# Dealing gathered row columns to the stretches of an expert mixer, and how far ahead they are fetched

## The chip, the cores and the metric

The kernel runs on one NeuronCore of one Trainium2 chip. The metric is the device time of one execution in microseconds; three runs of the kernel before are known. PE is TensorE, DVE VectorE, ACT ScalarE, POOL GpSimd, SP SyncE.

## The reference

One layer of a hybrid decoder for 336 tokens (256 prompt, 64 sample, 16 meta): a Conformer convolution branch and a Mamba-2 branch, joined and projected, and after them a PEER expert mixer. The change touches the mixer alone:

```python
def peer_block(xb, w_q, keys, U, V):
    q = (xb @ w_q).reshape(T, PEER_HEADS, 2, D_KEY // 2)
    s = jnp.einsum('thcd,hckd->thck', q, keys).astype(jnp.float32)
    s1, i1 = lax.top_k(s[:, :, 0], PEER_TOPK)
    s2, i2 = lax.top_k(s[:, :, 1], PEER_TOPK)
    ...
    sc, f = lax.top_k(cand, PEER_TOPK)
    ids = (jnp.take_along_axis(i1, f // PEER_TOPK, axis=-1) * N_KEYS
           + jnp.take_along_axis(i2, f % PEER_TOPK, axis=-1))
    g = jax.nn.softmax(sc, axis=-1)
    act = jax.nn.gelu(jnp.einsum('thkd,td->thk', U[ids], xb).astype(jnp.float32), approximate=False)
    w = (g * act).astype(xb.dtype)
    return jnp.einsum('thk,thkd->td', w, V[ids])
```

There are 8 heads with 16 experts each, so 128 experts a token out of 16384; U and V have 16384 rows of 1024.

## The kernel before, in words

The mixer treats its 320 tokens in two ways, side by side.

**Dense tokens.** 176 tokens go through all experts. The table U is read as 128 blocks of 128 experts (`u_block`, 512 KB each, tile `eraw`, fetched on SP's queue): PE multiplies a block with the tokens (L1272, tile `pj`), ACT applies gelu into S (L1274). Then V is read as 128 blocks (`v_block`), and PE adds S times a block into the accumulators `va` (L1366). Blocks are written here as U0 to U127 and V0 to V127. Between the two, S is weighted: `g_step` takes 8 tokens at a time, DVE builds one-hot tiles `oh` (L1293, L1294, L1296), PE multiplies them into `pg` (L1301), DVE multiplies `pg` into S (L1308). There are 22 such groups of 8 tokens for the first half of the experts (groups 0 to 21) and 22 for the second (22 to 43). Two `oh` buffers exist, so group n + 2 is built after group n is done.

**Gathered tokens.** 128 tokens (and 16 more, packed into 16 extra columns) fetch just the rows they need. A *column* is one expert for each of 128 partitions: `gather` has POOL issue an indirect DMA (L1083) of 128 rows of 8 KB, a U row and a V row side by side, into tile `wuv`. `pick_dot` has DVE take the dot product with the U half (L1195), ACT apply gelu and the gate (L1197, L1198, tile `scg`); `pick_sum` has DVE add the V half to `ygat` or `acce` (L1203). There are 144 columns and five `wuv` buffers (UV). `pick_row(n)` does the dot of column n and the sum of column n - 1; before the dot, `ahead(n)` issues the gathers that are wanted by then and not yet issued.

**What sets the order.** A `Feed` hands out such tasks between blocks: each block adds credit, and tasks are written into the program as the credit allows. There are four stretches: U0 to U87 beside the topk of the dense tokens (44 columns), U88 to U127 beside groups 0 to 21 (30), V0 to V63 beside groups 22 to 43 (42), and V64 to V126 beside nothing else (29 tasks: 28 columns and the last sum). A scheduler then settles each engine's row of instructions, so that a task need not stand where it was written. A gather issued at U88 or later also waits for a block's matmul:

```python
steps = ustep[SB:] + vstep
if len(steps) > LEAD:
    tc.add_manual_dep(i_.ins, steps[-1 - LEAD], ...)
```

that is, the block four before the one last written (LEAD is 4). SP fetches blocks into a ring of eight slots. Behind V126 `finish` normalizes and writes the gathered tokens, and `finish_dense` the others.

Of the kernel before, what the change touches and what calls it, by code (L numbers as in the profile page):

```python
# [42 lines left out]
NCOL = NPICK + (NPICK // XQ if NX else 0)  # L43
# [4 lines left out]
SB = 88  # L48
HB = 64
KTILES = ((0, NGAT), (128, 128), (256, 64))  # L50
NU = (44, 30, 42)
LM = (0.05, 0.05, 0.1, 0.5, 0.999)
LOW = 400
NW0 = 3
RB = 4
OH = 2
UV = 5
GLAG = 14
PLACE = (38, 50)
LASTP = 126  # L60
# [75 lines left out]
def body(tc, ia, oa, stop=None):  # L136
    nc = tc.nc
    with ExitStack() as top:
# [58 lines left out]
        def pj(name="pj"):  # L197
            return ps.tile([128, PJ], F32, name=name, tag="pj", bufs=3)[:, :T]
# [754 lines left out]
        def spread(row):  # L953
            u = gp.tile([128, 2 * D], F32, name="wuv", bufs=UV)[:, :D]
            nc.sync.dma_start(u, bass.AP(tensor=row.tensor, offset=row.offset, ap=[[0, 128], [1, D]]))
            return u
# [122 lines left out]
        ustep, vstep = [], []  # L1079

        def gather(c):
            u = gp.tile([128, 2 * D], F32, name="wuv", bufs=UV)
            i_ = nc.gpsimd.indirect_dma_start(out=u, out_offset=None, in_=ia["peer_uv"],  # L1083
                                              in_offset=bass.IndirectOffsetOnAxis(ap=gid[:, c:c + 1], axis=0))
            steps = ustep[SB:] + vstep
            if len(steps) > LEAD:
                tc.add_manual_dep(i_.ins, steps[-1 - LEAD], mybir.DependencyInfo(mybir.DependencyClass.Sync,
                                                                          mybir.DependencyReason.DATA),
                                  reason="rows after blocks")
            return u  # L1090

        def ahead(n):
            for i_ in range(n, min(n + UV - 1, NCOL)):
                if i_ not in pend:
                    pend[i_] = gather(COLS[i_])

        for j in range(16):
            w = weight(ia["w_q"], j)
            p = pj()
            proj(p[:, :T2], w, rows(ah[:, :, :T2], al[:, :, :T2]))  # L1100
            qT = qp.tile([128, T], F32, name="qT", bufs=3)
            nc.scalar.copy(qT[:, :T2], p[:, :T2])
            p = misc([128, 3, NK], "psc")
            for i, (t0, L) in enumerate(KTILES):
                nc.tensor.matmul(p[:L, i], qT[:, t0:t0 + L], keys[:, j, :], start=True, stop=True)  # L1105
                s_ = sall[:, i - 1, j] if i else kp.tile([128, NK], F32, name="sco", bufs=9)
                nc.scalar.copy(s_[:L], p[:L, i])
                if i == 0:
                    top16(sv[i], si[i], s_[:L], j)
            if j % (2 * HG) == 2 * HG - 1:  # L1110
                heads(j // 2 - HG + 1)
            if j == 2 * HG - 1:
                ahead(0)
# [77 lines left out]
        def pick_dot(n):  # L1191
            ahead(n)
            c, u = COLS[n], pend[n]
            w = scg[:, c:c + 1]
            nc.vector.scalar_tensor_tensor(u[:, :D], u[:, :D], 1.0, x2m if c < NPICK else x2e,  # L1195
                                           op0=OP.mult, op1=OP.mult, accum_out=w)
            nc.scalar.activation(w, w, AF.Gelu)  # L1197
            nc.scalar.activation(w, w, AF.Copy, scale=ggw[:, c:c + 1])  # L1198

        def pick_sum(n):  # L1200
            c, u = COLS[n], pend.pop(n)
            a_ = ygat if c < NPICK else acce
            nc.vector.scalar_tensor_tensor(a_, u[:, D:], scg[:, c:c + 1], a_, op0=OP.mult, op1=OP.add)  # L1203

        def group_sum():
            for c_ in range(2):
                p = misc([128, 512], "pgo")
                cs = slice(c_ * 512, c_ * 512 + 512)
                nc.tensor.matmul(p[:NX], C(f"sel{NX}"), acce[:, cs], start=True, stop=True)
                nc.scalar.copy(x2e[:NX, cs], p[:NX])  # L1210

        def pick_row(n):
# [4 lines left out]
            if n:  # L1217
                pick_sum(n - 1)
            if NX and n == XAT + NCOL - NPICK + GLAG:
                group_sum()  # L1220
# [3 lines left out]
        def take(n):  # L1224
            t = ops[:n]
            del ops[:n]
            return t

        def mixin(a_, b_):
            out, na, nb = [], len(a_), len(b_)  # L1230
            for q, t in enumerate(a_):
                out.append(t)
                out += b_[q * nb // na:(q + 1) * nb // na]
            return out

        t1, t2 = topk_tasks(1), topk_tasks(2)
        bg = mixin(t1[:-1] + t2[:-5] + t1[-1:] + t2[-5:-1], take(NU[0] - 4)) + take(4) + t2[-1:]

# [71 lines left out]
        def g_tasks(half):  # L1310
            return [(2.8, lambda t=t: g_step(half, t)) for t in range(0, ND, GT)]
# [8 lines left out]
        Sm.append(s1p.tile([128, 128 - SB, ND], F32, name="S1"))  # L1320
        feed = Feed(mixin(g_tasks(0), take(NU[1])), 128 - SB - 2)
        for b in range(SB, 128):
# [50 lines left out]
        def finish_dense():  # L1373
            yd = gp.tile([128, KD, ND], F32, name="nd")
            sqd = gp.tile([128, KD, ND], F32, name="sqd", tag="wuv", bufs=UV)
            pr = pj("prd")
# [11 lines left out]

        feed = Feed(mixin(g_tasks(1), take(NU[2])), HB - 2)
        for b in range(HB):  # L1390
# [109 lines left out]
```

## Time and profile before

| | |
|---|---|
| median of three runs | 1370.71 us (1370.0 to 1375.5) |
| the profiled execution | 1375.22 us, span 1373.5 |
| PE busy | 1319.4 us (96%), granted clock 0.983 |
| DVE, ACT, POOL busy | 1017.6, 526.4, 581.7 us |
| DMA | 382.05 MB, mean 278 GB/s; columns 151.00 MB on q0, blocks and the rest 227.46 MB on q1 |
| first U block, first V block, end of the last V block | 622.6, 996.3, about 1363 us into the span |

Busy times are sums over the whole span and say little about a stretch; the columns matter only from 622 us on, so the profile is read there, stretch by stretch. Matmuls of blocks are f32, and one of the program stands as two records in the profile: 16 records are one block. A wait is told as "engine, tile, line <- what ended it: us in total, times, longest".

### The profile page before, as it was taken

How to read it: one execution, taken by the hardware profiler on the slowest of the kernel's cores; microseconds unless marked ns; L12 is line 12 of the kernel's file. 1: busy time of each engine (PE TensorE's matmuls, PEld its weight loads, DVE VectorE, ACT ScalarE, POOL GpSimd, SP SyncE). 2: the span in 40 equal slices, each digit the busy share in tenths (PEclk: the TensorE clock that was granted, in tenths of full speed). 3: DMA queues.
4: the chain of work that ended last, by engine and by line, in shares of the span. 5: the costliest groups of instructions: out<-in, count | busy, mean ns of one | idle time of the engine just before them, and what ended most of it. 6: DMA issues, size and time to landing. Idle time of an engine off the chain costs nothing.

```text
span 1373.5 us, 24602 instructions
## 1 busy us (share of the span) xinstructions
PE 1319.4 (96%) x9324; PEld 1250.6 (91%) x9324; DVE 1017.6 (74%) x2340; ACT 526.4 (38%) x1393; POOL 581.7 (42%) x492
## 2 busy tenths in 40 slices
PE   9999999999999999998999988999999999987997
PEld 7888888888889999898998988999999999976897
DVE  7898777887866346799999885668787777766543
ACT  6777777777666434442222121111111111111101
POOL 2477776786746667542212331123222212344110
PEclk9999999999999999999999998999999999999999
DMA  6445545445344445439999999899999999999993
GB/s 237 160 127 171 166 160 162 142 149 187 108 142 127 150 154 165 148 114 380 398 413 393 409 416 362 288 416 363 372 416 415 380 377 390 395 417 416 414 412 113
DMA packets 87094, 382.05 MB, mean 278 GB/s; under 512 B 10144, under 2 KB 15648, under 8 KB 66368
## 3 DMA queue, kind: packets, MB, share of 16 engines
q1 hardware_dynamic: 65056, 227.46, 45.7%
q0 software_dynamic: 20736, 151.00, 27.3%
q10 hardware_dynamic: 1184, 2.02, 0.4%
q8 instruction: 73, 1.20, 0.3%
q14 instruction: 45, 0.37, 0.1%
HBM read 367.41 MB, written 13.03 MB: 277 GB/s over the span
## 4 chain that ended last, share of the span: by engine, by line
PE 77%; DVE 12%; DMA 8%; ACT 2%; issue 1%; POOL 0%; ACTq 0%; DVEq 0%
PE pj L150 30%; PE va L1366 19%; PE pj L1272 16%; DMA eraw<-in_vE_dram 5%; PE pg L1301 4%; PE pst L150 2%; DMA eraw<-in_uT_dram 2%; DVE wuv L1195 1%; DVE ygat L1203 1%; PE po L150 1%; PE py L150 1%; DVE pcv L473 1%; PE pdec L150 1%; PE ptr L155 1%; PE psc L1105 1%
## 5 line engine op out<-in xcount | busy, mean ns | idle before, releaser
L1083 POOL DMA_INDIRECT wuv<-in_peer_uv_dram,gid x144 | 183.0, 1271 | 523.4 <-DVE ygat L1203 159.7
L1272 PE MATMUL pj<-nd,eraw 128*128 128x176 f32 x2048 | 325.4, 320 | 11.5 <-DMA eraw<-in_uT_dram 7.6
L1366 PE MATMUL va<-S,eraw 128*128 128x176 f32 x2048 | 318.0, 315 | 18.9 <-DMA eraw<-in_vE_dram 18.9
L218 POOL TENSOR_TENSOR wl<-wraw,wh 128x1024 fp32r<-128x1024 f32 x111 | 267.2, 2408 | 149.7 <-ACT wh L217 78.0
L1366 PEld LDWEIGHTS va<-S,eraw 128*128 128x128 f32 x2048 | 307.6, 191 | 24.4 <-DMA eraw<-in_vE_dram 22.1
L1272 PEld LDWEIGHTS pj<-nd,eraw 128*128 128x128 f32 x2048 | 314.8, 195 | 13.5 <-ACT S L1274 8.8
L150 PE MATMUL pj<-ah,wh 128*128 128x336 f32 (+1 forms) x768 | 243.8, 329 | 0.7 <-ACT xnf L193 0.7
L150 PE MATMUL pj<-al,wh 128*128 128x336 f32 (+1 forms) x768 | 233.8, 318 | 0.0
L1203 DVE SCALAR_TENSOR_TENSOR ygat<-wuv,scg,ygat 128x1024 f32<-128x1024 f32 x128 | 163.9, 1280 | 57.8 <-ACT scg L1198 56.5
L1197 ACT ACTIVATE scg<-scg 128x1 f32<-128x1 f32 x144 | 29.0, 202 | 418.1 <-DVE wuv L1195 412.8
L1195 DVE SCALAR_TENSOR_TENSOR wuv<-wuv,x2m 128x1024 f32<-128x1024 f32 x128 | 156.0, 1218 | 42.6 <-DMA wuv<-in_peer_uv_dram,gid 42.6
L217 ACT CAST wh<-wraw 128x1024 fp32r<-128x1024 f32 x125 | 131.2, 1050 | 117.1 <-PE pj L150 79.9
L473 DVE SCALAR_TENSOR_TENSOR pcv<-ccat,vec,pcv 128x256 f32<-128x256 f32 x464 | 148.8, 379 | 17.1 <-ACT pcv L471 17.1
L150 PEld LDWEIGHTS pj<-ah,wh 128*128 128x128 f32 x768 | 147.1, 192 | 8.6 <-ACT xnf L193 2.7
L150 PEld LDWEIGHTS pj<-al,wh 128*128 128x128 f32 x768 | 146.5, 192 | 0.7
L150 PE MATMUL pj<-ah,wl 128*128 128x336 f32 (+1 forms) x768 | 137.0, 315 | 0.0
L150 PEld LDWEIGHTS pj<-ah,wl 128*128 128x128 f32 x768 | 120.5, 188 | 0.8 <-issue 0.7
L1274 ACT ACTIVATE S<-pj 128x176 f32<-128x176 f32 x128 | 37.6, 312 | 157.3 <-PE pj L1272 155.2
L1301 PE MATMUL pg<-oh 128*128 128x64 bf16 x1056 | 74.9, 242 | 0.0
L1308 DVE TENSOR_TENSOR S<-S,pg 128x192 f32<-128x192 f32 (+1 forms) x66 | 31.6, 506 | 56.9 <-PE pg L1301 56.9
L1301 PEld LDWEIGHTS <-oh 128*128 128x128 bf16 x1056 | 70.9, 117 | 2.2
L487 DVE SCALAR_TENSOR_TENSOR pj<-mcat,vec,pj 128x360 f32<-128x360 f32 x96 | 56.3, 588 | 3.6 <-ACT pj L485 3.6
(366 smaller groups left out, 1703.4 us busy)
## 6 DMA issues: line engine op xcount, KB each, us to landing
eraw<-in_uT_dram SPq DMA_DIRECT2D x128, 512.0 KB
eraw<-in_vE_dram SPq DMA_DIRECT2D x128, 512.0 KB
wraw<-in_w_in_dram SPq DMA_DIRECT2D x80, 512.0 KB
st<-in_state_dram SPq DMA_DIRECT2D x8, 1024.0 KB
out_ssm_s_dram<-st SPq DMA_DIRECT2D x8, 1024.0 KB
wraw<-in_w_mo_dram SPq DMA_DIRECT2D x16, 512.0 KB
wraw<-in_w_q_dram SPq DMA_DIRECT2D x16, 512.0 KB
wraw<-in_w_co_dram SPq DMA_DIRECT2D x8, 512.0 KB
```

The costliest lines, as they stand in the source:

```text
L150: i_ = nc.tensor.matmul(*a_, **kw)
L217: (nc.vector.tensor_copy if on_dve else nc.scalar.copy)(h, src)
L218: (nc.gpsimd if on_pool else nc.vector).tensor_tensor(l, src, h.bitcast(F32), op=OP.subtract)
L473: t = nc.vector.scalar_tensor_tensor(o, i_, wv, a_, op0=OP.mult, op1=OP.add)
L487: nc.vector.scalar_tensor_tensor(o, cat[:, w:w + n], wv, o, op0=OP.mult, op1=OP.add)
L1083: i_ = nc.gpsimd.indirect_dma_start(out=u, out_offset=None, in_=ia["peer_uv"], in_offset=bass.IndirectOffsetOnAxis(ap=gid[:, c:c + 1], axi ...
L1195: nc.vector.scalar_tensor_tensor(u[:, :D], u[:, :D], 1.0, x2m if c < NPICK else x2e, op0=OP.mult, op1=OP.mult, accum_out=w)
L1203: nc.vector.scalar_tensor_tensor(a_, u[:, D:], scg[:, c:c + 1], a_, op0=OP.mult, op1=OP.add)
L1272: i_ = nc.tensor.matmul(p[:, :ND], raw[:, k, :], nd[:, k, :], start=(k == 0), stop=(k == KD - 1))
L1274: nc.scalar.activation(Sv(b), p[:, :ND], AF.Gelu)
L1301: i_ = nc.tensor.matmul(pg[:, q, :], B[:, q // 4, :, q % 4], A[:, c_, q // 4, :, q % 4], start=(c_ == 0), stop=(c_ == 2))
L1366: i_ = nc.tensor.matmul(va[k // 2][:, k % 2], raw[:, k, :], Sv(b), start=False, stop=(b == 127), skip_group_check=True)
```

## The change

The columns are dealt 48, 30, 36 to the first three stretches, which leaves 31 tasks to the fourth. `ahead(n)` looked UV - 1 = 4 columns ahead (its own included) everywhere; now it does so while at most 64 V blocks are written (DEEP), and 2 from V64 on (NEAR): the dot of column n is written together with the gather of column n + 1.

```diff
-NU = (44, 30, 42)
+NU = (48, 30, 36)
 ...
 UV = 5
+DEEP = 4
+NEAR = 2
 ...
         def ahead(n):
-            for i_ in range(n, min(n + UV - 1, NCOL)):
+            for i_ in range(n, min(n + (DEEP if len(vstep) <= HB else NEAR), NCOL)):
                 if i_ not in pend:
                     pend[i_] = gather(COLS[i_])
```

Line numbers of the changed kernel are 2 higher in the mixer. POOL's row of instructions is unchanged; what its gathers wait for is not. Up to group 8 the rows of DVE, PE and ACT are unchanged too. The first place where they part is between groups 8 and 9. DVE's row there, before (a line with L1308 is a group's end, L1195 a column's dot, L1203 a sum):

```order
L1203 SCALAR_TENSOR_TENSOR ygat<-wuv,scg,ygat 128x1024
L1195 SCALAR_TENSOR_TENSOR wuv,scg<-wuv,x2m 128x1024
L1203 SCALAR_TENSOR_TENSOR ygat<-wuv,scg,ygat 128x1024
L1308 TENSOR_TENSOR S_7557<-S_7557,pg 128x64x8
L1293 TENSOR_TENSOR oh<-iorep,i2T 128x1024
L1294 TENSOR_TENSOR oh<-iorep,i1T 128x512
L1195 SCALAR_TENSOR_TENSOR wuv,scg<-wuv,x2m 128x1024
```

and now, at the same place:

```order
L1205 SCALAR_TENSOR_TENSOR ygat<-wuv,scg,ygat 128x1024
L1197 SCALAR_TENSOR_TENSOR wuv,scg<-wuv,x2m 128x1024
L1205 SCALAR_TENSOR_TENSOR ygat<-wuv,scg,ygat 128x1024
L1197 SCALAR_TENSOR_TENSOR wuv,scg<-wuv,x2m 128x1024
L1310 TENSOR_TENSOR S_7557<-S_7557,pg 128x64x8
L1295 TENSOR_TENSOR oh<-iorep,i2T 128x1024
L1296 TENSOR_TENSOR oh<-iorep,i1T 128x512
```

One more dot stands ahead of group 9's end: 55 columns instead of 54. Counted on in the same way it is 60 for 59 at group 14, 67 for 64 at group 19, 70 for 67 at group 21, and 108 for 105 at group 43, the last.

ACT's row just behind U88 holds the gelus of U blocks (S<-pj, with their number) and two small instructions for each column (`scg`). Before:

```order
L1197 ACTIVATE scg<-scg 128x1
L1198 ACTIVATE scg<-scg,ggw 128x1
L1274 ACTIVATE S_9217<-pj 128x176 x5
L1197 ACTIVATE scg<-scg 128x1
L1198 ACTIVATE scg<-scg,ggw 128x1
L1274 ACTIVATE S_9217<-pj 128x176 x2
```

and now, from the same instruction on:

```order
L1199 ACTIVATE scg<-scg 128x1
L1200 ACTIVATE scg<-scg,ggw 128x1
L1199 ACTIVATE scg<-scg 128x1
L1200 ACTIVATE scg<-scg,ggw 128x1
L1276 ACTIVATE S_9241<-pj 128x176
L1199 ACTIVATE scg<-scg 128x1
L1200 ACTIVATE scg<-scg,ggw 128x1
L1276 ACTIVATE S_9241<-pj 128x176 x3
```

The column that stood behind five more blocks now stands ahead of them, and the next behind one. Each column is some five blocks earlier against the U blocks from here to U127.

From V64 on DVE and ACT hold columns alone, in both kernels. There it is the gather's wait that moves, as the credits of the feed give it: column 120 waited for V62 and waits for V69, column 130 for V83 and V89, column 143, the last, for V110 and V115. On SP the row of the final norm's weights stands behind 123 V blocks instead of 122.

## The prediction

> **What bounds the kernel now.** I read the time by stage first: PE, the clock and the DMA beside one another, with cuts at U block 0, U block 88, V block 0, V block 64, the end of the starved stretch and V block 112. Columns: engine busy time (instructions), granted clock, DMA share, GB/s.
>
> ```profile
> core 0: us, PE busy (x) PEld busy (x) DVE busy (x) ACT busy (x) POOL busy (x), PEclk, DMA share, GB/s
> 622.60:878.00 255.40, 239.92 (x1656) 235.55 (x1655) 224.15 (x640) 57.96 (x211) 62.91 (x50) 0.96 0.98 389
> ...
> 878.00:996.20 118.20, 118.20 (x972) 117.57 (x970) 86.22 (x134) 21.81 (x82) 31.24 (x24) 1.00 0.96 372
> 996.20:1185.05 188.85, 188.85 (x1558) 186.25 (x1557) 145.08 (x239) 20.05 (x78) 41.01 (x38) 1.00 1.00 394
> 1185.05:1274.30 89.25, 72.50 (x450) 68.35 (x448) 60.48 (x73) 11.93 (x48) 37.20 (x23) 0.98 1.02 416
> 1274.30:1324.75 50.45, 48.33 (x320) 47.80 (x321) 25.17 (x30) 4.97 (x20) 10.63 (x9) 1.00 1.02 414
> 1324.75:1363.20 38.45, 38.45 (x260) 38.45 (x259) 12.28 (x23) 5.70 (x15) 1.74 (x1) 1.00 0.62 236
> ```
>
> PE is full from U88 to V63 and DMA is not: 372 and 394 GB/s against 416 later. From 1185.05 it turns round: DMA is at its ceiling and PE has holes. A block is 16 matmul records, so the stretch from 1185.05 (the burst, below) holds 450/16 = 28.1 V blocks in 89.25 us, the next 20 in 50.45, the last 16 (256 of its 260 are of blocks) in 38.45, or 2.40 us for a fed block. At 2.40 the burst's blocks would take 67.5 us and the next 48.0: **24.2 us of starvation** after V64. The waits from 1185 to 1275 say who starves:
>
> ```profile
> POOL wuv L1083 <- DMA wuv<-in_peer_uv_dram,gid: 28.9, 14, 3.7
> PEld va L1366 <- DMA eraw<-in_vE_dram: 19.5, 15, 2.3
> PE va L1366 <- DMA eraw<-in_vE_dram: 16.9, 15, 2.0
> ```
>
> PE waits for its blocks, and POOL for earlier row columns. The DMA queues in 1215 to 1275 show what they compete with (packets, MB, share; q0 is the columns, q1 the blocks):
>
> ```profile
> DMA packets 4580, 25.02 MB, mean 417 GB/s; under 512 B 511, under 2 KB 511, under 8 KB 2544
> q0 software_dynamic: 2290, 16.66, 67.2%
> q1 hardware_dynamic: 2288, 8.33, 34.4%
> ```
>
> Columns take two thirds of a full DMA. POOL's counts in the first fence are gathers alone (but for the last row's one), and show the burst: 23 columns go out beside its 28 blocks (1.2 blocks each), then 9 beside 20 (2.2 each, near the pace that the feed asks for). Of 144 columns 32 start after V64, so 112 before it; the program by then had asked for up to 119. The columns arrive late at V64 and are made up at once, since their waits on blocks are long satisfied.
>
> Prices. A column is 128 x 8 KB = 1.049 MB, a block 0.524 MB; at 416 GB/s 2.52 and 1.26 us. As a test, from V64 to the start of the last gather (V110, 46 blocks): 32 x 2.52 + 46 x 1.26 = 138.6 us of DMA beside 46 x 2.40 = 110.4 of PE, an excess of 28.2, against 24.2 seen. So about 4 us are absorbed by blocks fetched ahead.
>
> **The change, part by part.** *Deal up to U88 (48 for 44): nothing.* DVE, PE and ACT stand in the same order through one-hot group 8, at U88: there DVE's topk work sets the pace (busy 224.15 of 255.40 us), and columns wait behind it whatever the feed asks. Without that cover four columns would cost DVE 4 x 2.5 = 10 us. Only gathers 50 to 53 lose their wait on blocks U88 to U92. POOL's order is the same throughout.
>
> *U88 to V64 (36 for 42 in V0 to V63, but 4 more ahead): three columns come forward.* In this stretch a column is tied to blocks by ACT's queue: its gelu stands behind the gelus of U blocks. DVE's row shows it, as does the last group, where 105 columns stand ahead before and 108 now (counted in the order):
>
> ```profile
> 878.24 0.69 DVE L1308 TENSOR_TENSOR S<-S,pg 128x512 f32<-128x512 f32 x1 [2.54 <-PE pg L1301]
> 889.09 1.23 DVE L1195 SCALAR_TENSOR_TENSOR wuv<-wuv,x2m 128x1024 f32<-128x1024 f32 x1 [4.76 <-DMA wuv<-in_peer_uv_dram,gid]
> 906.28 1.28 DVE L1203 SCALAR_TENSOR_TENSOR ygat<-wuv,scg,ygat 128x1024 f32<-128x1024 f32 x1 [4.73 <-ACT scg L1198]
> 910.95 0.69 DVE L1308 TENSOR_TENSOR S<-S,pg 128x512 f32<-128x512 f32 x1 [0.36 <-PE pg L1301]
> L1308 DVE TENSOR_TENSOR S<-S,pg x66: 344/480/689, 806.6 to 1176.0; 128x512 f32<-128x512 f32 x22, 128x192 f32<-128x192 f32 x22, 128x320 f32<-128x320 f32 x22
> ```
>
> Between the first and the last of the four (groups 8 and 9) DVE has 5 dots before and 6 now, and group 9 ends at U97 instead of U101. Room on DMA: at 416 GB/s the two stretches from 878 to 1185.05 could carry 49.2 and 78.6 MB and carry 44.0 and 74.4, 9.4 MB free; three columns need 3.1. So PE's blocks should not suffer: 0, at worst the whole 3 x 2.52 = 7.6 us, if the free time lies where no column can use it. Room on DVE: its waits in 878 to 996.2, and the price of a dot and a sum:
>
> ```profile
> DVE ygat L1203 <- ACT scg L1198: 14.2, 6, 4.7
> DVE S L1308 <- PE pg L1301: 11.3, 10, 2.5
> L1203 DVE SCALAR_TENSOR_TENSOR ygat<-wuv,scg,ygat 128x1024 f32<-128x1024 f32 x128 | 163.9, 1280 | 57.8 <-ACT scg L1198 56.5
> L1195 DVE SCALAR_TENSOR_TENSOR wuv<-wuv,x2m 128x1024 f32<-128x1024 f32 x128 | 156.0, 1218 | 42.6 <-DMA wuv<-in_peer_uv_dram,gid 42.6
> ```
>
> Three columns are 3 x (1.22 + 1.28) = 7.5 us, against 11.3 in which DVE waits for PE. That is tight, since groups 10 to 16 follow closely: I charge **1 us** of PE waiting for one-hots (0 to 4; no gain here, since PE was full).
>
> *V64 on: two ahead instead of four.* The dot of column n now issues only gather n+1. By the feed's credits gathers 114 to 116 are still issued the old way; from 117 on gather n waits for block 2n - 171: V63, V65, and so on to V115 for 143 (V110 before). A late column no longer lets four gathers loose at once. By V64 29 gathers remain (32 less 3). From V64 to V115 DMA owes 29 x 2.52 + 51 x 1.26 = 137.3 us beside 51 x 2.40 = 122.4 of PE: 14.9 over, less the 4 absorbed: **11 us of starvation left** in place of 24.2, a gain of 13. The pace of two blocks a column alone costs 2 x 1.26 + 2.52 = 5.04 us against 4.80, 6 us over 26 columns; the rest is the start, where about two columns too many are due. Bounds: with the ring as empty at V64 as it is later nothing is absorbed, 15 left, gain 9; counting landings instead of issues I get 14. With two more columns done by V64, 6 left, gain 18.
>
> That byte price leans on 416 GB/s. The Trainium skill, "DMA: Bandwidth & Descriptors", section "Where 436 GB/s comes from", says that for HBM to SBUF the memory's share of one core, about 358 GB/s, binds. By that figure, as an estimate, column and block would cost 2.93 and 1.46 us and the debt would be 159.4, 37 over PE; 33 of starvation against 24.2 would make the change 9 us slower, near 1380. By that rule the trace does not agree: 417 GB/s held through 60 us above, so this way gets no chance of its own.
>
> *The end.* The tail hangs on the last column only if that comes late:
>
> ```profile
> 1320.75 1.90 POOL L1083 DMA_INDIRECT wuv<-in_peer_uv_dram,gid  x1 [3.83 <-PE va L1366]
> 1330.41 1.23 DVE L1195 SCALAR_TENSOR_TENSOR wuv<-wuv,x2m 128x1024 f32<-128x1024 f32 x1 [2.11 <-DMA wuv<-in_peer_uv_dram,gid]
> 1332.25 1.28 DVE L1203 SCALAR_TENSOR_TENSOR ygat<-wuv,scg,ygat 128x1024 f32<-128x1024 f32 x1 [0.60 <-ACT scg L1198]
> 1346.53 0.43 DVE L1345 COPY wraw<-ygat 128x512 f32<-128x512 f32 x1 [12.99 <-PE va L1366]
> 1362.80:1373.40 10.60, 3.26 (x19) 2.46 (x17) 5.45 (x15) 2.06 (x7) 0.00 (x0) 0.75 0.19 68
> ```
>
> Issue to end of sum is 12.8 us, 5.3 blocks: V120.3 when issued at V115. The first row of finish ran at 1346.53, (1346.53 - 1324.75)/2.40 = 9.1 blocks after V112, V121.1. So it fits with 2 us to spare: nothing, and 0 to 3 if that cover is gone. SP fetches the final norm's row one block later (behind V122), still ahead of its use. The last 10.6 us stay.
>
> *Sum.* +1 - 13 = **-12 us**. The profiled execution took 1375.22 us (span 1373.5 and 1.7 around it), 4.5 above the median of 1370.71; the same difference on the median gives **1359 us**. What is late next is still DMA after V64.
>
> **Rivals.** *The last stretch is fed nearly whole.* If four or five columns more are done by V64, DMA owes under 5 us: gain 18 to 24, 1347 to 1353. For it: DVE is only 77% busy in V0 to V63. Against: it waits there by its order, which moves three columns and no more.
>
> *Three columns forward, paid at once.* If they starve PE between U97 and V0, where DMA share is already 0.96, the 7.6 us come back: -13 + 7.6 = -5, about 1365, no measurable change. If they do not come forward at all, only the later last gather remains: 5 blocks of 2.40 - 1.26 each, 5.7 us gained, also 1365. For both: DVE's waits on ACT (14.2 us in 6), which can eat the lead; against: 9.4 MB of free DMA.
>
> *Slower: two ahead is too near.* The place is V64 to V115. Issue to dot took 9.7 us at the last gather; two columns ahead cover 2 x 4.80 = 9.6. If two in flight then really bound, with a time under load of some 13.5 us (an estimate: the burst's 89.25/23 = 3.9 us a gather, with three to four on the way), a column would take 6.75 us and the last of 27 would come 27 x 1.95 = 53 us later; 24 of freed starvation and some 4 of spare time come off: about +25, 1396. It decides once issue to dot exceeds about 12 us throughout. Against: the gathers wait for a block's matmul and a buffer, not for a dot, and five buffers remain.
>
> **How the numbers follow.** Forecast, gain 7 to 17: 0.58. Fed nearly whole: 0.10. Paid at once or never forward: 0.24. Two ahead too near: 0.08. The range runs from a gain of 20 (most of the second case) to none at all past the third: 1350 to 1370; below and above lie about 2 in 10. 0.5% (6.9 us, about what a measurement of this kernel can tell from no change) puts the first two cases at faster, 0.68, the third at same, 0.24, the last at slower, 0.08.
>
> **What would show it.** In the profile after, the stretch from V64 to V112 should take some 125 to 130 us instead of 139.7; gathers started by V64 should be about 115; after it they should come one per 4.8 to 5.0 us with no run at 3.76; waits of PE for V blocks should fall from 19.5 + 16.9 to under half; and U88 to V64 should stay within 2 us of 307.05 with PE full. I am wrong if PE shows waits for one-hots or for U blocks between U97 and V0, if gathers by V64 are still 112, or if DMA stays at 416 GB/s with PE starved as long as before.

## The result, and the profile after

| | before | after |
|---|---|---|
| median | 1370.71 us (1367.81 to 1375.5) | 1358.54 us (1357.92 to 1361.79, five runs) |
| ratio to before, 95% interval | | 0.9914 (0.9897 to 0.9932) |
| profiled execution | 1375.22 us, span 1373.5 | 1359.33 us, span 1357.6 |

The change gains 12.2 us on the medians (9.3 to 14.1 by the interval); 12 were forecast. First the stages of the kernel after, cut as before: U block 0, U88, V0, V64, the end of what is left of the starved stretch, V112. Columns: busy time (instructions) of PE, PEld, DVE, ACT and POOL, granted clock, DMA share, GB/s. The rows from 1181.55 on: the first 31 blocks from V64, V64 to V112 in one piece, V64 to the end of the last V block; the last row is the tail.

```profile
core 0: us, PE busy (x) PEld busy (x) DVE busy (x) ACT busy (x) POOL busy (x), PEclk, DMA share, GB/s
622.60:874.50 251.90, 238.55 (x1658) 234.06 (x1656) 224.29 (x641) 58.37 (x211) 67.08 (x53) 0.97 1.00 403
874.50:992.90 118.40, 118.40 (x972) 117.65 (x970) 93.54 (x143) 22.86 (x88) 29.72 (x24) 1.00 0.98 384
992.90:1181.55 188.65, 188.65 (x1557) 186.12 (x1556) 147.01 (x242) 20.55 (x80) 44.25 (x39) 1.00 0.99 392
1181.55:1265.00 83.45, 76.94 (x502) 74.56 (x501) 49.14 (x59) 9.45 (x38) 23.80 (x18) 1.00 1.02 413
...
1181.55:1308.20 126.65, 118.30 (x771) 114.64 (x770) 70.95 (x85) 13.93 (x56) 34.94 (x27) 1.00 1.02 414
1181.55:1347.25 165.70, 157.20 (x1028) 152.97 (x1027) 88.53 (x114) 20.62 (x75) 38.68 (x30) 1.00 0.95 385
...
1347.00:1357.60 10.60, 3.16 (x18) 2.35 (x16) 5.35 (x15) 2.07 (x7) 0.00 (x0) 0.85 0.19 68
```

From U88 to V64 nothing moved: 118.40 + 188.65 = 307.05 us, to the digit what it was, with PE full. V64 to V112 fell from 139.7 to 126.65. The same piece of the kernel before, V64 to the end of the last V block in one row:

```profile
1185.05:1363.20 178.15, 159.28 (x1028) 154.60 (x1027) 97.92 (x126) 22.60 (x83) 49.57 (x33) 0.99 0.93 376
```

178.15 became 165.70: 12.4 us, the whole gain of the medians. The other 3.5 us by which the profiled spans differ (15.9) lie ahead of U88 (255.40 against 251.90). They do not go with the change: e2_near below, whose order and waits up to U88 are those of the kernel before, took 251.3 us there, and all eleven profiled executions lie between 249.4 and 255.4.

Below, *starvation* is the stretch from V64 to the end of the last V block less 152.9 us, its length when every block is there in time (run e6_half shows it: 152.80 with PE full). By that measure it was 25.2 and is 12.8.

The waits between 1181 and 1271 us after (engine, tile, line, what ended the wait, us in total, times, longest):

```profile
POOL wuv L1085 <- PE va L1368: 39.6, 10, 5.3
DVE wuv L1197 <- DMA wuv<-in_peer_uv_dram,gid: 23.9, 19, 5.5
...
PEld va L1368 <- DMA eraw<-in_vE_dram: 8.3, 8, 1.4
POOL wuv L1085 <- DMA wuv<-in_peer_uv_dram,gid: 7.4, 4, 1.8
...
PE va L1368 <- DMA eraw<-in_vE_dram: 6.7, 8, 1.1
```

PE's waits for V blocks went from 19.5 + 16.9 to 8.3 + 6.7. POOL waited 28.9 us for earlier columns; now it waits 39.6 for a V block's matmul, so the pace is set by blocks. DMA's queues between 1211 and 1271 us (packets, MB, share; q0 columns, q1 blocks):

```profile
DMA packets 5075, 24.95 MB, mean 416 GB/s; under 512 B 566, under 2 KB 566, under 8 KB 3497
...
q0 software_dynamic: 1775, 12.91, 52.1%
q1 hardware_dynamic: 3298, 12.01, 49.8%
```

DMA is as full as it was (416 against 417), but the blocks' half has grown from 8.33 MB to 12.01. POOL's row from V64 on shows a short burst that is left, and then the pace:

```profile
1197.39 1.91 POOL L1085 DMA_INDIRECT wuv<-in_peer_uv_dram,gid  x1 [1.84 <-DMA wuv<-in_peer_uv_dram,gid]
1201.14 1.91 POOL L1085 DMA_INDIRECT wuv<-in_peer_uv_dram,gid  x1 [1.84 <-DMA wuv<-in_peer_uv_dram,gid]
1204.89 1.91 POOL L1085 DMA_INDIRECT wuv<-in_peer_uv_dram,gid  x1 [1.84 <-DMA wuv<-in_peer_uv_dram,gid]
1208.64 1.90 POOL L1085 DMA_INDIRECT wuv<-in_peer_uv_dram,gid  x1 [1.84 <-DMA wuv<-in_peer_uv_dram,gid]
1215.86 0.94 POOL L1085 DMA_INDIRECT wuv<-in_peer_uv_dram,gid  x1 [5.32 <-PE va L1368]
...
1255.42 0.94 POOL L1085 DMA_INDIRECT wuv<-in_peer_uv_dram,gid  x1 [2.82 <-DVE wuv L1197]
1260.19 0.94 POOL L1085 DMA_INDIRECT wuv<-in_peer_uv_dram,gid  x1 [3.83 <-PE va L1368]
```

Four gathers still follow one another at 3.75 us, each behind an earlier column's landing; each starts 0.76 us after the sum of the column five earlier, which frees its buffer. From 1215.86 on it is the block: gather n, from 124 to 143, starts 0.7 to 0.8 us after the first matmul of block V(2n - 171), the block that the prediction gives. That holds also where the profile names a sum or a dot as what ended the wait: their buffers had then been free for 4 us or more.

Last, the bytes. From V64 to the end of q0's last packet, before and then after, the row of the stretch and the two queues:

```profile
1185.13:1329.90 144.77, 125.91 (x805) 121.22 (x804) 88.09 (x106) 17.40 (x70) 47.84 (x32) 0.99 1.02 415
q0 software_dynamic: 4850, 35.28, 59.0%
q1 hardware_dynamic: 6783, 24.72, 42.4%
```

```profile
1181.62:1325.00 143.38, 134.88 (x879) 130.73 (x878) 78.93 (x94) 15.42 (x62) 36.87 (x29) 1.00 1.02 414
q0 software_dynamic: 4416, 32.12, 54.3%
q1 hardware_dynamic: 7426, 27.07, 47.0%
```

At 1.049 MB a column, 33.6 columns were owed at V64 and now 30.6 are: three came forward, although 112 gathers were out and now 116, since those last out had not landed. The last column lands when PE has taken 54.9 blocks (879/16) instead of 50.3, 4.6 later. At 0.524 MB a block, 51.6 blocks were fetched meanwhile and 47.1 before, so the ring gave up 3.3 blocks and 3.2. A column is 2.52 us of DMA, and a block of delay is worth 2.39 - 1.26 = 1.13: 3.0 x 2.52 + 4.6 x 1.13 = 12.8 us, against the 12.4 that the stretch lost.

### The profile page after: what moved, and what is told of

It is laid out like the page before. It is cut to its first block, busy times and chain, and to the rows that moved or that the text cites. A ratio compares the mean times of both kernels' runs of the same rounds, so it can differ in the third digit from the quotient of the medians.

```text
span 1357.6 us, 24599 instructions
## 1 busy us (share of the span) xinstructions
PE 1316.2 (97%) x9324; PEld 1247.7 (92%) x9324; DVE 1017.4 (75%) x2340; ACT 526.4 (39%) x1393; POOL 576.2 (42%) x492
## 4 chain that ended last, share of the span: by engine, by line
PE 74%; DVE 12%; DMA 11%; ACT 2%; issue 1%; POOL 0%; ACTq 0%; DVEq 0%; SPq 0%
PE pj L152 30%; PE va L1368 16%; PE pj L1274 14%; DMA eraw<-in_vE_dram 7%; PE pg L1303 4%; DMA eraw<-in_uT_dram 3%; PE pst L152 2%; DVE wuv L1197 1%; DVE ygat L1205 1%; PE po L152 1%; PE py L152 1%; DVE pcv L475 1%; PE pdec L152 1%; PE psc L1107 1%; PE ptr L157 1%
## 5 line engine op out<-in xcount | busy, mean ns | idle before, releaser
L1085 POOL DMA_INDIRECT wuv<-in_peer_uv_dram,gid x144 | 178.0, 1236 | 522.9 <-DVE ygat L1205 203.8
L1205 DVE SCALAR_TENSOR_TENSOR ygat<-wuv,scg,ygat 128x1024 f32<-128x1024 f32 x128 | 163.9, 1280 | 48.7 <-ACT scg L1200 48.5
L1310 DVE TENSOR_TENSOR S<-S,pg 128x192 f32<-128x192 f32 (+1 forms) x66 | 31.6, 506 | 54.9 <-PE pg L1303 54.8
```

## The experiments

All are edits of the kernel after, but for e5_nowait4. The *reach* is how many columns ahead `ahead(n)` looks from V64 on (NEAR). Ratios are to the kernel before, run on the same chip in the same set (medians 1370.43 for the first four runs, 1370.84 for the next four, 1370.54 for the last).

| run | median, us | ratio (95% interval) | starvation, us | gathers started by U88 / V0 / V64 |
|---|---|---|---|---|
| before | 1370.71 | 1 | 25.2 | 50 / 74 / 112 |
| after | 1358.54 | 0.9914 (0.9897 to 0.9932) | 12.8 | 53 / 77 / 116 |
| e1_deal | 1362.44 | 0.9954 (0.9940 to 0.9968) | 16.3 | 53 / 77 / 116 |
| e2_near | 1365.89 | 0.9975 (0.9963 to 0.9987) | 20.1 | 50 / 74 / 112 |
| e3_v42 | 1363.23 | 0.9955 (0.9942 to 0.9968) | 19.1 | 53 / 77 / 115 |
| e4_near1 | 1357.22 | 0.9906 (0.9892 to 0.9921) | 9.7 | 53 / 77 / 116 |
| e5_nowait4 | 1368.41 | 0.9977 (0.9966 to 0.9989) | 21.6 | 53 / 75 / 113 |
| e6_half | 1347.34 | 0.9827 (0.9807 to 0.9848) | 0 | 53 / 77 / 116 |
| e7_pin2 | 1354.47 | 0.9886 (0.9868 to 0.9904) | 9.6 | 53 / 77 / 115 |
| e8_late | 1354.14 | 0.9878 (0.9858 to 0.9898) | 9.0 | 53 / 77 / 116 |
| e9_lead10 | 1352.71 | 0.9868 (0.9848 to 0.9889) | 8.5 | 53 / 77 / 116 |

**e1_deal: the deal alone.**

```diff
-NEAR = 2
+NEAR = 4
```

> The deal 48, 30, 36 alone, four columns ahead everywhere. Theory (bytes owed after V64, less the time of PE until the last gather's block): columns come forward as in the changed kernel, about 116 gathers by V64, but the last gather waits for V111, not V115. 28 or 29 columns and 47 blocks owe 130 to 132 us beside 113 of PE, 16 of starvation in place of 24: 7 to 9 us faster than before. Rival one, the shorter look-ahead does it all by ending the burst: within 2 us of before, with gathers at 3.8 us each behind V64. Rival two, the deal does it all: 12 us faster.

V64 to the end of the last V block:

```profile
1179.10:1348.30 169.20, 157.41 (x1028) 152.96 (x1027) 88.71 (x114) 20.62 (x75) 40.95 (x30) 1.00 0.93 376
```

8.0 us gained, starvation 16.3, as expected: the columns that are out earlier are worth two thirds of the change (the deal also puts the last gather one block later, at V111).

**e2_near: the shorter reach alone.**

```diff
-NU = (48, 30, 36)
+NU = (44, 30, 42)
```

> The look-ahead of two from V64 on alone, with the deal 44, 30, 42. Theory: 112 gathers by V64 as before, the last one behind V114 instead of V110. 32 columns and 50 blocks owe 143.6 us beside 120 of PE, less the 4 absorbed: 19 to 20 of starvation, 4 to 5 us faster than before. Rival one, ending the burst is what counts: 10 us faster or more. Rival two, the deal does it all: within 2 us of before.

The same stretch:

```profile
1179.60:1352.60 173.00, 158.03 (x1028) 152.98 (x1027) 97.90 (x126) 22.61 (x83) 48.93 (x33) 1.00 0.95 387
```

4.5 us gained. No column comes earlier (112 by V64, as before); only the gathers behind V64 are spread. 8.0 + 4.5 = 12.5 against 12.2 for both: within the intervals the two parts add.

**e3_v42: 42 columns beside V0 to V63, with the 48 and the short reach kept.**

```diff
-NU = (48, 30, 36)
+NU = (48, 30, 42)
```

> 48, 30, 42 instead of 48, 30, 36, with two ahead from V64 on: six more columns are asked for before V64, but DVE, ACT and PE stand in the same order up to the last one-hot group, with 108 columns ahead of it. The waits of gathers up to 122 are on blocks before V58, so they are let loose at V64, and the last gather waits for V113. Theory: the debt hardly changes, 28 or 29 columns and 49 blocks, 12 to 14 us of starvation: 10 to 12 us faster than before, 1 to 2 slower than the changed kernel, with a burst behind V64 all the same. Rival, the burst itself costs the time: 5 us faster than before or less, with starvation as before. Other rival, the deal 36 in place of 42 moves columns by itself: then the count by V64 differs from 116 by more than two.

It gained 7.2 us where I expected 10 to 12, and starves 19.1 us instead of 12 to 14, so this was a miss. Up to the last one-hot group the order is that of the kernel after, 108 dots, and the gathers by V64 are one fewer, so the rival that counts columns does not hold either. The rival of the burst asked for 5 us or less and starvation as before (25.2); it is not met either: the run lies between the two. What differs is the pace behind V64. The stretch in four pieces (to V76, V76 to V88, V88 to V112, the rest):

```profile
1179.10:1208.90 29.80, 28.85 (x195) 28.58 (x193) 20.55 (x25) 3.98 (x16) 14.21 (x9) 1.00 1.01 411
1208.90:1254.10 45.20, 31.84 (x192) 28.62 (x193) 30.05 (x37) 5.97 (x24) 18.39 (x10) 1.00 1.02 417
1254.10:1312.80 58.70, 57.64 (x385) 57.39 (x386) 25.51 (x31) 4.97 (x20) 14.30 (x10) 1.00 1.02 413
1312.80:1351.10 38.30, 38.30 (x258) 38.30 (x258) 14.71 (x26) 6.19 (x17) 2.67 (x2) 1.00 0.60 233
```

Most of the starving is done by 1254: 24.2 blocks (387/16) take 75.0 us where 57.8 would do (2.39 us each), since 19 gathers go out beside them. In the kernel after 31.4 blocks pass beside the first 18 (x502 and x18 in 83.45 us). Behind 1254 PE is fed, yet DMA stays at 413 GB/s. The queues of e3_v42 between 1254.1 and 1312.8 us:

```profile
q1 hardware_dynamic: 3907, 14.24, 60.5%
q0 software_dynamic: 1374, 9.94, 41.1%
```

14.24 MB are 27.2 blocks, and PE took 385/16 = 24.1: some three blocks went into the ring early, 3 x 1.26 = 4 us of DMA time, while columns were still owed. From V64 to the end of q0's last packet, as shown above for the kernel after:

```profile
1179.13:1324.70 145.57, 130.19 (x850) 126.47 (x849) 81.12 (x97) 15.91 (x64) 47.81 (x30) 1.00 1.02 414
q0 software_dynamic: 4463, 32.51, 54.2%
q1 hardware_dynamic: 7582, 27.60, 47.2%
```

Only 0.4 MB of columns more are owed than in the kernel after, 0.9 us of DMA (the 116th gather starts 1.8 us behind V64 instead of 0.8 ahead of it, hence 115). The last column lands 1.8 blocks earlier against PE (850/16 = 53.1 instead of 54.9), 1.8 x 1.13 = 2.0 us. And PE took 53.1 blocks while 52.6 were fetched: the ring gave up 0.5 of a block instead of 3.3, 2.8 x 1.26 = 3.5 us. Together 6.4 us, and starvation differs by 6.3. So the 36 earns its place by the pace behind V64, not by columns that it moves, and the ring that fills while columns are owed is over half of what the 42 costs. This account was made after the run, from its trace; no other run varies the pace of the fed part by itself.

**e4_near1: the reach cut to one.**

```diff
-NEAR = 2
+NEAR = 1
```

> 48, 30, 36 and no look-ahead from V64 on: the dot of column n issues its own gather. The last gather waits for V117. Theory: 28 columns and 53 blocks owe 137 us beside 127 of PE, 7 to 10 of starvation: 14 to 16 us faster than before, 2 faster than the changed kernel, less up to 3 if the last sum, at about V122.5, comes late for the finishing rows. Rival, too near a fetch makes the columns the bound: the last sum well behind V124 and a time above that of the changed kernel by more than 3 us.

13.2 us gained, a little under the 14 to 16 expected, with starvation 9.7 as expected, and the tail did not grow. Fetching closer to the turn is not too near. By starvation it is better than the kernel after (9.7 against 12.8), since the last gather waits for V117 instead of V115; the medians, 1357.22 and 1358.54 from separate sets of runs, do not tell the two apart.

**e5_nowait4: the kernel before, with four gathers let go early.** Only the wait on U88 to U92 is taken from gathers 50 to 53; deal and reach are those of before.

```diff
-            if len(steps) > LEAD:
+            if len(steps) > LEAD and not 50 <= c < 54:
```

> The kernel before (44, 30, 42, four ahead everywhere), but gathers 50 to 53 do not wait for blocks U88 to U92, as they do not in the changed kernel. Question: does the early start of these four alone bring the columns forward, or must DVE's order follow (106 dots stand ahead of the last one-hot group here, 105 before, 108 in the changed kernel)? Theory, the order carries the lead: 53 gathers by U88, but 112 to 113 by V64, starvation of 22 to 25 us, 0 to 3 us faster than before. Rival, the early gathers alone: 115 or 116 by V64, 16 of starvation, 7 to 9 faster.

2.4 us gained, as expected. From U0 of the kernel before (622.60; here U0 began at 621.75, and U0 to U88 took 249.8 us) to U88, and V64 to the end of the blocks:

```profile
622.60:871.50 248.90, 236.37 (x1650) 232.36 (x1649) 223.21 (x635) 58.00 (x210) 66.56 (x53) 0.97 1.01 407
...
1178.90:1353.40 174.50, 157.72 (x1027) 152.99 (x1027) 95.41 (x123) 22.11 (x82) 52.16 (x32) 1.00 0.93 377
```

53 gathers are out by U88, as in the kernel after, but the lead is lost on the way: 75 by V0 and 113 by V64. An early start alone is kept for one column of three. The lead that is kept is that of the dots in DVE's row: 106 stand ahead of the last group here, 105 before and 108 after. From gather 59 up to V64 nearly every gather, in this run and in both kernels, starts 0.76 us after the end of the sum five columns earlier: a column's buffer comes free only with its sum.

**e6_half: half the bytes for the late columns.** Columns from 117 on fetch a 4 KB U row instead of the 8 KB pair, and the sum uses it in place of the V half, so that the V half is left out of the computation. Order, waits and counts stay.

```diff
+            late = len(vstep) > HB
+            if late:
+                half.append(c)
-            i_ = nc.gpsimd.indirect_dma_start(out=u, out_offset=None, in_=ia["peer_uv"],
+            i_ = nc.gpsimd.indirect_dma_start(out=u[:, :D] if late else u, out_offset=None,
+                                              in_=ia["peer_h"] if late else ia["peer_uv"],
```

> The changed kernel, but every column from 117 on fetches only the U half of its rows, 4 KB instead of 8 (its sum then adds what stands in that half; the V half is left out). Order, waits and counts stay. Theory, bytes owed starve PE: a late column costs 1.26 us of DMA instead of 2.52, 27 x 1.26 = 34 us less is owed, starvation after V64 falls from 12.7 to 0 or 1, some 12 us faster than the changed kernel, 24 faster than before. Rival, the number of gathers or POOL's issue holds the blocks up: starvation of 6 or more stays, under 7 us faster than the changed kernel.

```profile
1182.30:1335.10 152.80, 152.80 (x1027) 152.80 (x1026) 87.73 (x114) 20.62 (x75) 33.73 (x30) 1.00 0.88 324
```

23.5 us gained; PE is full from V64 to the end. With the same order and the same waits, the bytes of the late columns are what starves PE. The number of gathers or of packets is not the cause: from V64 to the last column's landing q0 moved 4399 packets, against 4416 in the kernel after. This row also gives the length of the fed stretch.

**e7_pin2: more columns ahead of the last group.** The reach is 1, and the one-hots of the second half's groups are held behind the dot that is third from last as written.

```diff
-NEAR = 2
+NEAR = 1
...
+            if half:
+                after(i_, dots[-1 - 2])
```

> 48, 30, 36 with each late column issuing its own gather (no look-ahead from V64 on), and in V0 to V63 the one-hots of a group are built only behind the dot of the column third from the last one written so far: 76 instead of 74 dots ahead of group 22, 111 instead of 108 ahead of the last, which moves from V59 to V63. Theory: DMA has room for three more columns there (392 GB/s of 416 over 189 us is 4.5 MB), so 116 land by V64 instead of 113, and starvation falls by 7 to 8 us from 9.6; DVE's tighter order costs PE 1 to 3 us before V64: 17 to 20 us faster than before. Rival, DVE becomes late with the one-hots: PE waits 7 us or more between V0 and V64 and nothing is won over the kernel without look-ahead (13 faster than before).

V0 to V64, and the rest:

```profile
990.30:1179.60 189.30, 189.15 (x1559) 186.13 (x1558) 147.04 (x245) 19.86 (x78) 41.07 (x38) 1.00 1.00 394
1179.60:1342.10 162.50, 156.64 (x1028) 152.94 (x1027) 89.27 (x116) 21.12 (x77) 36.55 (x30) 1.00 0.96 388
```

16.4 us gained, a little under the 17 to 20 expected, and for another reason than mine. PE stayed full up to V64, so DVE was not late; but no column more is out by V64 (115), and starvation is 9.6, not 2 to 3. 111 dots stand ahead of the last group, but that group has moved from V59 to V63: the count at a fixed block is the same. Against e4_near1, which has the same reach, the starvation is equal. The two medians differ by 2.8 us, from separate sets of runs. The profiled executions differ by 2.3, and 2.2 of that lie between U0 and U88 (252.1 and 249.9 us), which neither edit touches; I put nothing down to the pinning.

**e8_late: the gathers behind V64 held back further.** Reach 1, and behind V64 a gather waits for the block two back instead of four.

```diff
-                tc.add_manual_dep(i_.ins, steps[-1 - LEAD], ...
+                tc.add_manual_dep(i_.ins, steps[-1 - (LEAD if len(vstep) <= HB else 2)], ...
```

> 48, 30, 36, no look-ahead from V64 on, and there a gather waits for the block two behind the last one written instead of four: the last gather waits for V119, its sum comes at about V123. Theory: two blocks more to pay the debt in, 7 to 8 us of starvation, 2 less than with V117; but the finishing rows need about 11 us and now start 9 to 10 before the end of the blocks, so the tail grows from 12.9 by 1 to 3 us: 12 to 15 us faster than before, no gain over V117. Rival, the tail has room left: tail 12.9, 15 to 16 faster. Rival, late columns bound the end: tail up by more than 4.

V64 to the end of the blocks, and DVE's row at the end (L1205 is the last sum, L1347 finish):

```profile
1180.00:1341.90 161.90, 156.65 (x1026) 152.83 (x1025) 88.35 (x114) 20.51 (x75) 35.82 (x30) 1.00 0.97 394
```

```profile
1331.27 1.28 DVE L1205 SCALAR_TENSOR_TENSOR ygat<-wuv,scg,ygat 128x1024 f32<-128x1024 f32 x1 [0.60 <-ACT scg L1200]
1332.74 0.43 DVE L1347 COPY wraw<-ygat 128x512 f32<-128x512 f32 x1 [0.19 <-DMA wuv<-in_fnorm_dram]
```

16.7 us gained where I expected 12 to 15, with starvation 9.0 where I expected 7 to 8: a miss on both, and the rival holds by which the tail has room left (15 to 16). The last gather now waits for V119, finish follows the last sum at once, and the blocks still end no later for it: 10.3 us lie behind them (1352.2 less 1341.9), as in the kernel after (1357.6 less 1347.25). Against e4_near1 starvation is 0.7 us less, which does not carry the 3.1 us between the medians of separate sets.

**e9_lead10: in addition, the gathers up to V64 let go earlier.** They wait for the block ten back instead of four.

```diff
-            if len(steps) > LEAD:
+            lead = 10 if len(vstep) <= HB else 2
+            if len(steps) > lead:
```

> As the kernel whose last gather waits for V119, but until V64 a gather waits for the block ten behind the last one written instead of four. Question: what caps the columns landed by V64, the waits on blocks or DVE's order (which is the same here, 108 dots ahead of the last one-hot group)? Theory, the waits hold POOL back (80 us of its waiting in V0 to V63 was for V blocks in the kernel with pinned one-hots): 114 to 115 land by V64 instead of 113.3, starvation after V64 falls from 9.0 to 5 to 7 us, 18 to 20 us faster than before. Rival, DVE's order and the five buffers cap it: landed within half a column of 113.3, starvation 8 to 10, 16 to 17 faster.

POOL's waits between 990 and 1180 us, in e8_late and then in e9_lead10 (whose lines are one higher):

```profile
POOL wuv L1085 <- DVE ygat L1205: 68.1, 13, 9.3
POOL wuv L1085 <- PE va L1368: 41.9, 10, 7.0
```

```profile
POOL wuv L1085 <- DVE ygat L1206: 69.9, 14, 9.3
POOL wuv L1085 <- PE va L1369: 40.1, 9, 7.0
```

17.8 us gained, between the 16 to 17 of the rival and the 18 to 20 of the theory. The theory fails all the same: still 116 gathers by V64, and starvation 8.5 where it asked for 5 to 7. By starvation the rival holds (8 to 10). POOL waits where it did, for a sum to free a buffer. That goes also for the 40 us that the profile puts down to a block: in both runs gathers 59 to 112 start 0.76 us after the end of the sum five columns earlier (but for one, 1.12 us), whatever name the wait has. Six blocks more of freedom move nothing, so DVE's order and the five buffers cap the count. At 1352.71 this is the best version that computes all of the output; its interval overlaps that of e8_late, so the two are not told apart. Both beat the kernel before, and each interval lies under the ratio of the kernel after (0.9914), though that of e8_late just touches its interval; against the kernel after itself they were not timed.

## Why the prediction came out right, point by point

- **The sum.** -12 was forecast, -12.2 came, closer than the interval can tell. V64 to the end of the last block lost 12.4 us, against the 13 of the sum, and the 1 us charged against it did not come; that two small misses offset is luck. Of the starvation, 11 was to be left. By the measure of the prediction (V64 to V112 at 2.40 us a block) 126.65 less 771/16 x 2.40 is 11.0; by mine, over all 64 blocks, 25.2 became 12.8. The central claim, that bytes owed behind V64 set this stretch, was tested by e6_half and holds.
- **What carries it.** The sum did not part the gain between deal and reach. e1_deal and e2_near do: 8.0 and 4.5. Counted from V64 to the last landing in their traces, as above, e1_deal owes 3.1 columns less than the kernel before (32.01 MB against 35.28) and lands its last column 0.6 blocks later, 8.5 us; e2_near owes the same (35.20 MB) and lands it 3.9 blocks later, 4.4 us.
- **Gathers by V64.** About 115 were expected, 116 were started; in bytes just three columns came forward, as forecast.
- **Place of the three columns: wrong for the fetches.** "Deal up to U88: nothing" and three columns forward between U88 and V64 was the step. The counts of gathers show 53 gathers against 50 already at U88, and 63 against 62 from there to V64. The rows are POOL's gathers before and after, with POOL's count in brackets, up to U88 and from U88 to V64:

```profile
602.00:878.00 276.00, 62.91 (x50) 0.96 0.95 372
878.00:1185.05 307.05, 72.25 (x62) 1.00 0.98 385
```

```profile
602.00:874.50 272.50, 67.08 (x53) 0.97 0.97 385
874.50:1181.55 307.05, 73.96 (x63) 1.00 0.99 389
```

I had listed the means, "only gathers 50 to 53 lose their wait", and given it no weight. In the kernel before they started 10.7 to 19.2 us after their buffers were free, now 0.3 us. That brings the bytes forward. DVE's row then keeps them forward, and here the forecast was right: DVE has 143 instructions from U88 to V0 instead of 134, three columns of three. The first half alone does not do it: e5_nowait4 keeps one column of three. The second half alone was not run.
- **1 us for late one-hots: 0.** U88 to V64 is 307.05 us in both. Of the three columns only one more gather falls in this stretch, so most of the bytes were paid before it.
- **About 4 us absorbed: not a constant.** It is the ring's contents: 3.2 blocks given up by the time the last column lands in the kernel before, 3.3 after, and 3.6 to 3.8 in e1_deal, e2_near, e4_near1 and e5_nowait4. e3_v42, where the ring refills in a fed part, gives up 0.5 and starves 19.1 us with nearly the columns of the kernel after.
- **"No run at 3.76": wrong in part.** One of four gathers at 3.75 us is left, right behind V64, where the first credits of the last stretch meet columns that are late. After it the spacing is 4.8 to 7.5 us. PE's waits fell to 15.0 of 36.4 us, under half, as expected.
- **The end: nothing.** Last sum at 1327.36, finish at 1330.62, and the last row, 10.6 us, as long as before.
- **The rivals.** Three columns paid at once: excluded by 307.05 with PE full; never forward: excluded by the counts. Two ahead too near: e4_near1, with one ahead, is not slower. Fed nearly whole: needs the bytes of e6_half; e9_lead10, the best with all bytes, keeps 8.5 us.
- **The bandwidth rule.** The Trainium skill ("DMA: Bandwidth & Descriptors", "Where 436 GB/s comes from") gives about 358 GB/s, a memory stack's rate divided by its two cores, as what binds from HBM to SBUF, by which this change would have lost time. With that no trace here agrees: this one core held 413 to 417 GB/s over stretches of 45 to 127 us in the kernel after and in e3_v42.

One reading of the deal was loose throughout: that "36 for 42" was an edit of the columns beside V0 to V63. In the order the count ahead of the last group is 108 for 48, 30, 36 and for 48, 30, 42, and 105 for 44, 30, 42: the 48 moves columns, the 36 only sets the credit behind V64.

## What to carry to other kernels

Where a stretch has DMA at its ceiling and PE waiting, write down the bytes owed up to the last transfer that counts against the time PE needs for the same blocks; the excess, less what the prefetch ring gives up meanwhile, is the stall, and it falls with every byte moved to where DMA has room and with every block by which the last transfer may come later. An earlier issue is kept only as far as the instructions that free its buffer move too. Read what a wait is put down to against the times: here a constant distance from the sum that frees the buffer showed what a block's name had hidden. The extra transfers are best spread evenly: a burst starves PE first, and a slack pace after it lets DMA fill the prefetch ring while transfers are still owed.

## What the hardware showed that I had not expected

- The stretch U0 to U88 took 249.4 to 255.4 us in the eleven profiled executions (255.4 before, 251.7 after), though POOL, DVE, PE and ACT have the same order there in all of them. The spread is half of what this change gains, so one profile beside another misstates the change (15.9 us here, where the medians give 12.2). What sets it is open. The waits that gathers 50 to 53 lose do not sort the runs: e2_near keeps them and took 251.3, e6_half is without them and took 253.8. Nor does the mean granted clock: 0.99 in e1_deal goes with 250.7, 0.98 in e6_half with 253.8, 0.97 in e3_v42 with 249.4.
- Queued columns take twice the share of blocks: 67.2% to 34.4% in the kernel before, where gathers followed one another. The packets of the same rows say why: 2290 and 2288. While both queues have work they move packet for packet, and a column's packets carry twice the bytes (16.66 MB against 8.33). So it is in e3_v42 from 1210 to 1254 us (1678 and 1681 packets) and in e5_nowait4 from 1200 to 1250 us (1904 and 1902). Where the issue of columns waits for blocks, as in the kernel after, the packets are 1775 and 3298 and the shares 52.1% and 49.8%, at the same 416 GB/s.
